# Casts and bank copies issued ahead of the exponentials in attention, and a transform's tiles loaded behind the modulation's row blocks

## The chip, the cores and the metric

One core of one Trainium2 chip runs the whole program in one launch. The metric is device microseconds per execution, the median over several runs. TensorE is written PE, its weight loads PEld, VectorE DVE, ScalarE ACT, GpSimd POOL and SyncE SP; the DMAs of this kernel are issued from SP's queue, in order.

## The reference, cut to what matters

One layer of a transformer-like block on 512 latent tokens (width 1024) and 256 context tokens, all in fp32:

```python
sh1, sc1, g1, sh2, sc2, g2 = split(silu(c) @ w_mod + b_mod, 6)      # and the same from c_ctx for the context
h  = rms_norm(x, norm1_g) * (1 + sc1) + sh1                          # hc likewise from ctx
qa, ka, va, hy, qd, kd, vd = split(h @ w_in)                         # ka, va, kd, vd of hc too
ya = attention(qa, [ka_c; ka], [va_c; va])                           # 4 heads of 64, 2 key heads, 768 keys
yd = softmax(q1 k1) v - lam * softmax(q2 k2) v                       # 4 heads, values 128 wide
yh = x2 * conv(h2, x1 * conv(h1, v))                                 # long convolutions by FFT, filters from a small MLP
x  = x + g1 * (concat(norm(ya), norm(yh), norm(yd)) @ w_out)
x  = x + g2 * conv_glu(rms_norm(x, norm2_g) * (1 + sc2) + sh2)       # up to 2 x 2816, down to 1024
```

Two details matter below. The modulation `silu(c) @ w_mod` has to be complete before the first row of h exists. The long convolution is done with matrices of cosines and sines ("dft" tiles), first on the filters (`spectrum("s", ..)` and `spectrum("d", ..)`), later on the data.

## The kernel before, in words

Nearly every product is done as three matmuls (`mm3`): both operands are split into a high part, made by a cast on ACT (`hi_of`, L72), and a remainder, made by a subtraction on DVE or POOL (`lo_of`, L80). The three matmuls then stand at L83, L84 and L85. A weight tile thus costs a DMA, a cast of 128x1024 and a subtraction of 128x1024.

**First stage (L376 to L490).** The first 2048 columns of `w_mod` come as eight row blocks of 1 MB (`mod1_load`, L165, tile `mraw`, four buffers). `mod1(k)` (L249) multiplies block k into one PSUM bank; between these calls PE builds the filters (`filter_part`) and adds up their norms (`filter_norm`, L425). PE's order is written out by hand here (`manual_schedule` for PE alone); the order on ACT, DVE, POOL and SP is set by a planner from estimated times when the program is built, as far as data, buffers and `issue_after` allow. `load_dft(g)` (L263) loads 512 KB of cosine and sine matrices and splits them at once. After `mod1(7)` the bank is copied, transposed (`modT`, L257) and made into columns (`modc`, `gs1`). Then x, normalised, is transposed in eight pieces (`transposed`, L360), each modulated (`hm`), cast and split into `hTh`, `hTl`; the spectra of the filter sum stand between the pieces, the first of them in two halves, one of them ahead of `mod1(7)` (L450). `shy` streams the weights of the Hyena projection (`prep` casts and splits one).

**Projections (L500 to L925).** Hyena, then the eight q, k, v blocks `corder`. `mod2_step` (L746) takes one step of the other four modulation vectors: a DMA of 512 KB and a multiply-add on DVE; after every eighth step 16 small matmuls (`mc`, L768) sum over partitions, one call later, since `pause` lets one call pass. `MOD_AT` says how many calls go ahead of each weight unit. In the last block (ci = 7) the first three steps of attention are already done between the matmuls (`early_step`), PE and DVE in hand-written order.

**Attention (L1163 to L1215).** 16 steps of differential attention, then 16 of the grouped one; a step is 128 queries of one head. The loop counter n runs from 3. For n below LATE = 16 a step has two halves jj (the two softmaxes). For each: `front` does the scores on PE into one of two score banks (`ps_s`, 128x768) and then `exp_of` (L779): a maximum on DVE, an exponential on ACT. Around it stand, in program order: `combine(n-1)` (the two reciprocals and the mixing on POOL), `advance()` (one step of each running generator: splitting q and k of the next head, normalising a finished head, transposing it), `transposes(n-3, half)` (three transposes on PE into a bank `ps_t`, three of these in all, and their copy out on ACT, tiles `at`), and `values(n-5)`. PE, DVE and ACT all run in this hand-written order, so an instruction waits for every earlier one of its own engine:

```python
held[n] = front(n, 0)()              # scores, maximum, exponential of half 0
if on(D_C): combine(n - D_C, held[n - D_C])
advance()
if on(D_T): transposes(n - D_T, held[n - D_T][0], 0)
held[n] += front(n, 1)()
if on(D_T): transposes(n - D_T, held.pop(n - D_T)[0], 1)
if on(D_V): values(n - D_V)
```

**Tail of attention (L1205 to L1215).** The last head has to be copied, transposed, normalised (`finish_a`, L1014) and transposed again (`yTa`), one piece per `advance()`. Between these PE has 24 units of the output projection (`accumulate`, three matmuls of 512 columns each); `TAIL` says how many go ahead of each `advance()`. `wo_unit` (L1130) loads and splits a tile of `w_out`; `WO_LO` names the engine of the subtraction, one letter per tile. Tiles 3 to 7 are traced after the hand-written part (L1231).

Of the kernel before, what the change touches and what calls it, by code (L numbers as in the profile page):

```python
# [16 lines left out]
P = 128  # L17
WO_LO = "ppppvvvv"
# [9 lines left out]
TAIL = (2, 0, 0, 0, 0, 0, 7, 0, 0, 2)  # L28
# [16 lines left out]
def block_kernel(tc, x, ctxt, small, ffs, wmod1, wmod2, whyd, wqkvd, woutd, wupd, wdownd,  # L45
# [217 lines left out]
    def load_dft(g):  # L263
        if g < 2:
            stage = qk.tile([P, 4, 256], F32, tag=("yhn", "qa")[g], bufs=1, name=f"dft_{g}").rearrange("p a c -> p (a c)")
        else:
            stage = wp.tile([P, 1024], F32, tag="wr", bufs=3, name=f"dft_{g}")
        st = stage.rearrange("p (m a f) -> p m a f", m=2, a=2)
        dma(st, dftd[2 * g:2 * g + 2].rearrange("m (a p) f -> p m a f", p=P))
        h = dfp.tile([P, 2, 2, 256], F32R, name=f"dfh{g}")  # L270
        l = dfp.tile([P, 2, 2, 256], F32R, name=f"dfl{g}")
        hi_of(h, st, "a")
        lo_of(l, st, h, "v" if g < 2 else "p")
        for j in range(2):
            dft[names[2 * g + j]] = (h[:, j], l[:, j])
# [121 lines left out]
    load_dft(0)  # L397
    dma(coef, coefd.rearrange("(m p) c -> p m c", p=P))
# [4 lines left out]
    mod1_load(6)  # L403
    loaded = mod1_load(7)
    load_dft(1)
# [44 lines left out]
    spectrum("s", 0, (1,))  # L450
# [9 lines left out]
    with tc.issue_after(last[0].ins):  # L460
        shy.prep(0)
    mv = mod1_columns()
    dft["coT"] = dft["co"]
    dft["soT"] = dft["so"]
# [5 lines left out]
    for v in range(2):  # L470
        V.scalar_tensor_tensor(gs1[:, v], modc[:, 8:16, v], 1.0, cols[:, C_N1:C_N1 + 8], ALU.add, ALU.mult)
# [6 lines left out]
    for n in range(NK):  # L478
        next(tr)
        if n == 0:  # L480
            spectrum("s", 0, (0,))
        if n in (1, 3, 5):
            spectrum("s", (n + 1) // 2)
        if n == 5:
            with tc.issue_after(last[3].ins):
                shy.prep(1)
# [18 lines left out]
    for u in range(6):  # L505
        wh, wl = shy.get(u)
        if u == 2:
            load_dft(2)
# [237 lines left out]
    def mod2_step():  # L746

        if m2s.pop("pause", False):
            return
# [14 lines left out]
        if k == NK - 1:  # L764
            def due(a=m2s["a"]):
                t0 = m2s["ps"](f"mc{g}")
                for i in range(NK):
                    T_.matmul(t0[:, 2 * i:2 * i + 2], a[:, i * P:(i + 1) * P], ones[:, 0:2], start=True, stop=True)  # L768
                V.tensor_tensor(mcol[:, g], t0[:, 0:16:2], cols[:, C_BM + 8 * g:C_BM + 8 * g + 8], ALU.add)
            m2s["due"], m2s["pause"] = due, True  # L770
# [7 lines left out]

    def exp_of(p_, mx, s, stat):  # L779
        V.tensor_reduce(mx, s[:, :768], AX.X, ALU.max, negate=True)  # L780
        S.activation(p_, s[:, :768], AF.Exp, bias=mx, scale=1.0, accum_out=stat)
# [10 lines left out]
    def early_step(e):  # L792
# [11 lines left out]
        mx = cst.tile([P, 1], F32, tag="mxe", bufs=2, name=f"mxe{n}{jj}")  # L804
        exp_of(p_, mx, s, state["st0"][:, n, jj:jj + 1])
# [11 lines left out]
    for ci, ch in enumerate(corder):  # L817
# [6 lines left out]
        for u in range(2):  # L824
# [8 lines left out]
            for b, bank in enumerate(banks):  # L833
                th, tl = (hTh, hTl) if b < 2 else (cTh, cTl)
                for j in range(2):
# [6 lines left out]
                    if ci == 7:  # L842
# [5 lines left out]
                        if e % 3 == 0:  # L848
                            mod2_step()
# [164 lines left out]
    def finish_a(b, yps):  # L1014
# [15 lines left out]
        if b == 1:  # L1030
# [4 lines left out]
            for b_ in range(2):  # L1035
                yv = yna[b_].rearrange("p a j d -> p a (j d)")
                V.tensor_tensor(yv, yv, sa[:, 2].unsqueeze(2).broadcast_to([P, 4, P]), ALU.mult)
# [9 lines left out]
    def front(n, jj):  # L1047
# [3 lines left out]
        if kind == "a":  # L1051
            if jj:
                return lambda: []
# [9 lines left out]
        def rest():  # L1063
            mx = att.tile([P, 1], F32, tag="mx", bufs=4, name="mx" + nm)
            p_ = att.tile([P, 768], F32, tag="p", bufs=7, name="p" + nm)
            exp_of(p_, mx, s, stat)
            return [p_]
# [62 lines left out]
    def wo_unit(n_):  # L1130
# [10 lines left out]
        lo_of(l, r, h, WO_LO[n_])  # L1141
# [23 lines left out]
    while n < len(steps) + D_V:  # L1165
# [10 lines left out]
        if late:  # L1176
# [4 lines left out]
            if n - 1 in waiting:  # L1181
                held[n - 1] = waiting.pop(n - 1)()
# [9 lines left out]
        else:  # L1192
            held[n] = front(n, 0)()
# [5 lines left out]
            held[n] += front(n, 1)()  # L1199
            if on(D_T):  # L1200
                transposes(n - D_T, held.pop(n - D_T)[0], 1)
            if on(D_V):
# [304 lines left out]
```

## Time and profile before

| | |
|---|---|
| median of 3 runs | 807.86 us (805.63 to 809.38) |
| the profiled execution | 807.56 us, its span 805.8 us |
| PE busy | 774.5 us (96% of the span) |
| DVE, ACT, POOL busy | 476.9, 317.8, 194.6 us |
| granted clock of PE, mean | 0.991 |
| moved by DMA | 93.68 MB |

The span is the time from the first to the last instruction of the profiled execution. A row of the timeline reads: start, duration, engine, line, operation, output<-input, shape, count, and in square brackets how long the engine stood idle before it and which instruction ended that. Several equal instructions in a row are merged into one.

### The profile page before, as it was taken

The numbers are of one execution on the slowest core, as the hardware profiler recorded it, in microseconds if no ns is written. First come the engines' busy times: TensorE is split into PE (matmuls) and PEld (weight loads), VectorE is DVE, ScalarE is ACT, GpSimd is POOL, SyncE is SP. The second block draws the span as 40 slices with busy tenths as digits, with TensorE's granted clock in tenths as the row PEclk, the third lists the DMA queues.
The fourth block names the chain that finished last, engine by engine and source line by source line (L and its number), as shares of the span: only waits on it lengthen the run. The fifth ranks groups of instructions, "written<-read, shape, count | busy, mean of one in ns | idle before, by whom it ended". The sixth has DMA issues, their size and how long they took to land.

```text
span 805.8 us, 11143 instructions
## 1 busy us (share of the span) xinstructions
PE 774.5 (96%) x4355; PEld 655.1 (81%) x4355; DVE 476.9 (59%) x683; ACT 317.8 (39%) x546; POOL 194.6 (24%) x187
## 2 busy tenths in 40 slices
PE   8899999999989888899899999999999999999997
PEld 2278899999988777789689988888888888888886
DVE  5588659687767777776476785344444433332325
ACT  2576343223213678787243343323333332332220
POOL 0518036849821657421151000000000000000000
PEclk9799999999999999999999999999999999999999
DMA  8913311225675241501551372322232222223202
GB/s 325 393 51 112 105 54 53 79 79 179 214 218 161 66 104 29 144 27 53 171 171 54 113 245 86 105 104 83 101 105 90 93 99 84 100 85 104 79 27 104
DMA packets 30701, 93.68 MB, mean 116 GB/s; under 512 B 5639, under 2 KB 8022, under 8 KB 29625
## 3 DMA queue, kind: packets, MB, share of 16 engines
q1 hardware_dynamic: 30649, 92.98, 35.0%
q8 instruction: 34, 0.56, 0.3%
q14 instruction: 18, 0.15, 0.1%
HBM read 83.79 MB, written 2.10 MB: 107 GB/s over the span
## 4 chain that ended last, share of the span: by engine, by line
PE 81%; DVE 6%; DMA 4%; ACT 4%; POOL 2%; issue 1%; SPq 0%; ACTq 0%; DVEq 0%; POOLq 0%
PE u L84 5%; PE u L83 5%; PE u L85 5%; PE dn L85 5%; PE dn L84 5%; PE dn L83 5%; DMA mraw<-in_dram 4%; PE uv L83 2%; PE ua L85 2%; PE uv L84 2%; PE uv L85 2%; PE ua L83 2%; PE ua L84 2%; PE yd L1103 2%; PE o L85 2%; PE o L84 2%
## 5 line engine op out<-in xcount | busy, mean ns | idle before, releaser
L80 DVE TENSOR_TENSOR ul<-ur,uh 128x1024 fp32r<-128x1024 f32 x62 | 75.9, 1224 | 101.6 <-ACT uh L72 100.9
L72 ACT CAST uh<-ur 128x1024 fp32r<-128x1024 f32 x66 | 69.2, 1051 | 116.8 <-PE u L84 90.6
L83 PE MATMUL u<-h2h,uh 128*128 128x512 f32 (+1 forms) x224 | 81.3, 363 | 0.0
L85 PE MATMUL u<-h2h,ul 128*128 128x512 f32 (+1 forms) x224 | 80.4, 359 | 0.0
L84 PE MATMUL u<-h2l,uh 128*128 128x512 f32 (+1 forms) x224 | 80.4, 359 | 0.0
L84 PE MATMUL dn<-ul,gh 128*128 128x512 f32 x176 | 69.6, 397 | 0.0
L85 PE MATMUL dn<-uh,gl 128*128 128x512 f32 x176 | 69.6, 397 | 0.0
L83 PE MATMUL dn<-uh,gh 128*128 128x512 f32 x176 | 69.3, 397 | 0.0
L80 DVE TENSOR_TENSOR gl<-gT,gh 128x512 fp32r<-128x512 f32 x22 | 15.2, 690 | 60.1 <-ACT gh L72 60.1
L84 PEld LDWEIGHTS u<-h2l,uh 128*128 128x128 f32 x224 | 42.3, 189 | 6.3
L83 PEld LDWEIGHTS u<-h2h,uh 128*128 128x128 f32 x224 | 42.3, 189 | 6.2
L85 PEld LDWEIGHTS u<-h2h,ul 128*128 128x128 f32 x224 | 42.3, 189 | 6.2
L80 DVE TENSOR_TENSOR wl<-wr,wh 128x1024 fp32r<-128x1024 f32 x22 | 31.5, 1433 | 19.4 <-ACT wh L72 19.3
L763 DVE SCALAR_TENSOR_TENSOR macc<-mraw,sv,macc 128x1024 f32<-128x1024 f32 x28 | 37.4, 1335 | 8.1 <-DMA mraw<-in_dram 8.0
L72 ACT CAST gh<-gT 128x512 fp32r<-128x512 f32 x22 | 13.5, 620 | 70.1 <-PE dn L84 70.1
L83 PEld LDWEIGHTS dn<-uh,gh 128*128 128x128 f32 x176 | 33.2, 189 | 8.1
L85 PEld LDWEIGHTS dn<-uh,gl 128*128 128x128 f32 x176 | 33.2, 188 | 8.1
L84 PEld LDWEIGHTS dn<-ul,gh 128*128 128x128 f32 x176 | 33.2, 188 | 8.0
L72 ACT CAST wh<-wr 128x1024 fp32r<-128x1024 f32 x22 | 23.0, 1047 | 41.2 <-PE hy L84 8.2
L83 PE MATMUL uv<-h2h,uh 128*128 128x512 f32 x80 | 31.2, 391 | 0.2 <-ACT uh L72 0.2
L83 PE MATMUL ua<-h2h,uh 128*128 128x512 f32 x80 | 31.4, 392 | 0.0
L84 PE MATMUL uv<-h2l,uh 128*128 128x512 f32 x80 | 31.2, 390 | 0.0
(771 smaller groups left out, 2173.9 us busy)
## 6 DMA issues: line engine op xcount, KB each, us to landing
ur<-in_dram SPq DMA_DIRECT2D x66, 512.0 KB, 3.2
mraw<-in_dram SPq DMA_DIRECT2D x32, 512.0 KB, 4.5
wr<-in_dram SPq DMA_DIRECT2D x22, 512.0 KB, 3.3
mraw<-in_dram SPq DMA_DIRECT2D x8, 1024.0 KB, 11.8
or<-in_dram SPq DMA_DIRECT2D x8, 512.0 KB, 4.6
xo<-in_dram SPq DMA_DIRECT2D x6, 512.0 KB, 9.3
x<-in_dram SPq DMA_DIRECT2D x4, 512.0 KB, 5.8
out_dram<-x SPq DMA_DIRECT2D x8, 256.0 KB, 2.0
```

What stands on the lines that cost most here:

```text
L72: return S.copy(dst, src)
L80: return e.tensor_tensor(dst, src, f(hi), ALU.subtract)
L83: i0 = T_.matmul(o, ah, bh, start=start, stop=False)
L84: T_.matmul(o, ah, bl, start=False, stop=False)
L85: return i0, T_.matmul(o, al, bh, start=False, stop=stop)
L763: V.scalar_tensor_tensor(m2s["a"], r, sv[:, k:k + 1], m2s["a"], ALU.mult, ALU.add)
L1103: T_.matmul(o, Vt[2 + h][:, kt], at[:, kt], start=kt == 0, stop=kt == 5)
```

## The change

In the first stage it loads the two dft pieces later (the first behind row block 6, the second behind block 7), puts six matmuls on a zero tile where half of the first spectrum stood, and does the spectra whole, one behind every second transposed piece. In the modulation's second part it pauses one call longer after the second vector and moves the calls inside the last projection block. In attention it parts the maximum from the exponential: copies and casts traced between now go first on ACT. In the tail it gives 10 and 4 units where 7 and 2 stood, puts tile 3's subtraction on DVE, and holds the subtractions of tiles 4 to 7 behind the last scaling of the last head.

```diff
-WO_LO = "ppppvvvv"
+WO_LO = "pppvvvvv"
...
-TAIL = (2, 0, 0, 0, 0, 0, 7, 0, 0, 2)
+TAIL = (2, 0, 0, 0, 0, 0, 10, 0, 0, 4)
...
-        dma(st, dftd[2 * g:2 * g + 2].rearrange("m (a p) f -> p m a f", p=P))
+        dft["dma"] = dma(st, dftd[2 * g:2 * g + 2].rearrange("m (a p) f -> p m a f", p=P))
         h = dfp.tile([P, 2, 2, 256], F32R, name=f"dfh{g}")
         l = dfp.tile([P, 2, 2, 256], F32R, name=f"dfl{g}")
-        hi_of(h, st, "a")
-        lo_of(l, st, h, "v" if g < 2 else "p")
...
+        def split():
+            hi_of(h, st, "a")
+            lo_of(l, st, h, "v" if g < 2 else "p")
...
+        return split
...
     mod1_load(3)
-    load_dft(0)
-    dma(coef, coefd.rearrange("(m p) c -> p m c", p=P))
     mod1_load(4)
     for a in (2, 3):
         x_load(a)
     mod1_load(5)
-    mod1_load(6)
-    loaded = mod1_load(7)
-    load_dft(1)
+    loaded = mod1_load(6)
+    with tc.issue_after(loaded.ins):
+        split = load_dft(0)
+    with tc.issue_after(dft["dma"].ins):
+        split()
+        loaded = mod1_load(7)
+    with tc.issue_after(loaded.ins):
+        dma(coef, coefd.rearrange("(m p) c -> p m c", p=P))
+        split = load_dft(1)
+    loaded = dft["dma"]
...
-    spectrum("s", 0, (1,))
+    warm(6, "3")
     mod1(7)
...
-    with tc.issue_after(last[0].ins):
-        shy.prep(0)
...
-        V.scalar_tensor_tensor(gs1[:, v], modc[:, 8:16, v], 1.0, cols[:, C_N1:C_N1 + 8], ALU.add, ALU.mult)
+        ins = V.scalar_tensor_tensor(gs1[:, v], modc[:, 8:16, v], 1.0, cols[:, C_N1:C_N1 + 8], ALU.add, ALU.mult)
+    with tc.issue_after(ins.ins):
+        split()
...
         next(tr)
-        if n == 0:
-            spectrum("s", 0, (0,))
-        if n in (1, 3, 5):
-            spectrum("s", (n + 1) // 2)
-        if n == 5:
+        if n % 2:
+            spectrum("s", n // 2)
+        if n in (3, 5):
             with tc.issue_after(last[3].ins):
-                shy.prep(1)
+                shy.prep(n // 2 - 1)
...
-        if m2s.pop("pause", False):
+        if m2s.get("pause"):
+            m2s["pause"] -= 1
             return
...
-            m2s["due"], m2s["pause"] = due, True
+            m2s["due"], m2s["pause"] = due, 2 if g == 1 else 1
...
+    def max_of(mx, s):
+        V.tensor_reduce(mx, s[:, :768], AX.X, ALU.max, negate=True)
+
     def exp_of(p_, mx, s, stat):
-        V.tensor_reduce(mx, s[:, :768], AX.X, ALU.max, negate=True)
         S.activation(p_, s[:, :768], AF.Exp, bias=mx, scale=1.0, accum_out=stat)
...
-                        if e % 3 == 0:
+                        if e in (2, 4, 6, 8, 9):
                             mod2_step()
...
-                V.tensor_tensor(yv, yv, sa[:, 2].unsqueeze(2).broadcast_to([P, 4, P]), ALU.mult)
+                state["yna"] = V.tensor_tensor(yv, yv, sa[:, 2].unsqueeze(2).broadcast_to([P, 4, P]), ALU.mult)
...
         hi_of(h, r, "a")
-        lo_of(l, r, h, WO_LO[n_])
+        if n_ < 4:
+            lo_of(l, r, h, WO_LO[n_])
+        else:
+            with tc.issue_after(state["yna"].ins):
+                lo_of(l, r, h, WO_LO[n_])
...
-                held[n - 1] = waiting.pop(n - 1)()
+                held[n - 1] = waiting.pop(n - 1)()()
...
-            held[n] = front(n, 0)()
+            exps = front(n, 0)()
             if on(D_C):
                 combine(n - D_C, held[n - D_C])
             advance()
             if on(D_T):
                 transposes(n - D_T, held[n - D_T][0], 0)
-            held[n] += front(n, 1)()
+            held[n] = exps()
+            exps = front(n, 1)()
             if on(D_T):
                 transposes(n - D_T, held.pop(n - D_T)[0], 1)
+            held[n] += exps()
             if on(D_V):
                 values(n - D_V)
```

`issue_after(ins)` adds an edge of order from `ins` to each instruction traced in its block that runs on the engine of `ins`, and to no other. In the first stage the edges thus bind SP's queue alone, at the second split DVE alone. `front` now returns the scores' continuation in two calls, the first for the maximum, the second for the exponential; the steps from n = 16 on call both at once, as before.

## Rows read from the trace of the kernel before

**Rows 1.** The busy time of each engine in stretches of the span: length, then PE, PEld, DVE, ACT, POOL, the granted clock of PE, the DMA share and GB/s.
```profile
0.00:50.00 50.00, 41.57 (x160) 15.86 (x161) 31.25 (x60) 22.08 (x44) 12.88 (x23) 0.90 0.82 302
50.00:200.00 150.00, 150.00 (x1065) 140.22 (x1064) 113.70 (x165) 57.07 (x95) 81.14 (x81) 1.00 0.26 88
...
226.00:268.00 42.00, 38.29 (x298) 37.19 (x296) 27.91 (x39) 12.56 (x24) 8.24 (x7) 0.96 0.61 175
268.00:330.00 62.00, 51.51 (x314) 44.42 (x314) 46.82 (x87) 45.64 (x103) 40.66 (x33) 1.00 0.34 82
...
376.00:401.00 25.00, 22.70 (x122) 18.76 (x122) 10.00 (x15) 7.58 (x11) 3.61 (x3) 1.00 0.36 127
```

**Rows 2.** The timeline of PE in the first stage: matmuls on a zero tile (`warm`), filters (`f`), row blocks and norms (`modl`), the half spectrum (`ktC0s`, first row of six matmuls).
```profile
10.35 1.88 PE L205 MATMUL warm<-nil 128*128 128x448 bf16 x9
...
26.91 1.98 PE L413 MATMUL f<-fw3s,h 65*128 65x512 f32 x4
32.38 1.93 PE L251 MATMUL modl<-mraw,scol 128*32 128x512 f32 x8 [3.48 <-DMA mraw<-in_dram]
34.24 3.59 PE L425 MATMUL modl<-habs,ones 128*128 128x512 f32 x4
...
38.76 1.13 PE L425 MATMUL modl<-habs,ones 128*128 128x512 f32 x2
39.33 0.80 PE L83 MATMUL ktC0s<-fhsp,dfh 128*128 128x512 f32 x1
...
41.21 1.07 PE L251 MATMUL modl<-mraw,scol 128*32 128x512 f32 x8
```

**Rows 3.** A stretch of the first stage by itself, columns as in rows 1.
```profile
30.00:38.00 8.00, 5.62 (x16) 1.53 (x20) 4.32 (x6) 4.51 (x12) 5.11 (x8) 0.57 1.01 415
```

**Rows 4.** The timeline of SP's queue: when DMAs were issued (the duration is that of the issue, not of the transfer).
```profile
18.05 0.43 SPq L269 DMA_DIRECT2D dft<-in_dram  x1
18.58 4.35 SPq L168 DMA_DIRECT2D mraw<-in_dram  x3
...
37.34 0.38 SPq L619 DMA_DIRECT2D rope<-in_dram  x1
```

**Rows 5.** The timelines of ACT and DVE in the first stage: the cast and the subtraction of the first Hyena weight tile.
```profile
44.48 1.06 ACT L72 CAST wh<-wr 128x1024 fp32r<-128x1024 f32 x1
...
45.57 1.22 DVE L80 TENSOR_TENSOR wl<-wr,wh 128x1024 fp32r<-128x1024 f32 x1 [0.17 <-ACT wh L72]
```

**Rows 6.** The timeline of PE from 233 to 253 us: its waits in the last projection blocks.
```profile
236.49 1.92 PE L768 MATMUL mc<-ones,macc 128*128 128x2 f32 x16 [2.11 <-DVE macc L763]
247.68 0.50 PE L776 MATMUL se<-ks1d,qsd 128*128 128x512 f32 x1 [0.55 <-ACT pe L781]
252.54 0.50 PE L776 MATMUL se<-ks0d,qsd 128*128 128x512 f32 x1 [1.05 <-ACT pe L781]
```

**Rows 7.** DVE around the last of these waits, and the stretch behind the first of them (columns as in rows 1).
```profile
249.25 1.28 DVE L763 SCALAR_TENSOR_TENSOR macc<-mraw,sv,macc 128x1024 f32<-128x1024 f32 x1 [1.46 <-DMA mraw<-in_dram]
250.46 0.95 DVE L780 TENSOR_REDUCE mxe<-se 128x1 f32<-128x768 f32 x1
...
236.00:247.00 11.00, 10.51 (x74) 10.39 (x74) 7.32 (x11) 2.96 (x4) 0.00 (x0) 0.84 0.48 150
```

**Rows 8.** The timeline of PE in attention: the waits that ended with a copy or cast on ACT, and one of those that ended with an exponential (the first row).
```profile
271.45 0.50 PE L776 MATMUL sd10None<-ksX,X 128*128 128x512 f32 x1 [0.76 <-ACT pd03None L781]
...
279.17 0.55 PE L1086 MATMUL Td02None<-ident,pe 128*128 128x128 f32 x3 [1.21 <-ACT atd02None L72]
285.26 0.55 PE L1086 MATMUL Td03None<-ident,pd03None 128*128 128x128 f32 x3 [1.77 <-ACT atd02None L72]
...
311.17 0.55 PE L1086 MATMUL Td21None<-ident,pd21None 128*128 128x128 f32 x3 [1.67 <-ACT atd20None L72]
316.70 0.55 PE L1086 MATMUL Td22None<-ident,pd22None 128*128 128x128 f32 x3 [1.20 <-ACT ynd L991]
...
327.86 0.55 PE L1086 MATMUL Td31None<-ident,pd31None 128*128 128x128 f32 x3 [1.06 <-ACT atd30None L72]
329.12 0.66 PE L971 MATMUL yTd<-ident,ynd 128*128 128x128 f32 x4 [0.71 <-ACT atd30None L72]
```

**Rows 9.** ACT's queue in one of these steps, ahead of the wait at 285.26, and one row of a later step (a finished head's square).
```profile
282.74 0.90 ACT L781 ACTIVATE pd12None<-sd12None,mxd12None 128x768 f32<-128x768 f32 x1 [2.36 <-DVE mxd12None L780]
...
283.63 0.47 ACT L72 CAST khd<-kT1d 128x384 fp32r<-128x384 f32 x1
283.99 0.85 ACT L978 ACTIVATE Y<-yTh,cols 128x256 fp32r<-128x256 f32 x2
284.71 0.50 ACT L72 COPY atd02None<-Td03None 128x384 f32<-128x384 f32 x1
...
298.25 0.63 ACT L992 ACTIVATE ysqd<-ynd 128x512 f32<-128x512 f32 x1
```

**Rows 10.** The tail of attention: PE's first matmul of the seven units, its two waits, and the subtraction that DVE does ahead of the last head's sums.
```profile
382.02 0.48 PE L83 MATMUL o<-oh,Y 128*128 128x512 f32 x1
...
388.61 0.63 PE L971 MATMUL yTa<-ident,yna 128*128 128x128 f32 x4 [1.44 <-DVE yna L1037]
...
391.49 0.63 PE L971 MATMUL yTa<-ident,yna 128*128 128x128 f32 x4 [0.85 <-DVE yna L1037]
...
382.98 2.59 DVE L80 TENSOR_TENSOR ol<-or,oh 128x1024 fp32r<-128x1024 f32 x1
...
```

More of the change, by code (lines that the diff above doesn't have):

```diff
@@ L268, in load_dft @@
         st = stage.rearrange("p (m a f) -> p m a f", m=2, a=2)
-        dma(st, dftd[2 * g:2 * g + 2].rearrange("m (a p) f -> p m a f", p=P))
+        dft["dma"] = dma(st, dftd[2 * g:2 * g + 2].rearrange("m (a p) f -> p m a f", p=P))
         h = dfp.tile([P, 2, 2, 256], F32R, name=f"dfh{g}")
         l = dfp.tile([P, 2, 2, 256], F32R, name=f"dfl{g}")
-        hi_of(h, st, "a")
-        lo_of(l, st, h, "v" if g < 2 else "p")
-        for j in range(2):
-            dft[names[2 * g + j]] = (h[:, j], l[:, j])
+        def split():
+            hi_of(h, st, "a")
+            lo_of(l, st, h, "v" if g < 2 else "p")
+            for j in range(2):
+                dft[names[2 * g + j]] = (h[:, j], l[:, j])
+        return split
     ss = cst.tile([P, 6], F32, name="ss1")
@@ L459, in block_kernel @@
         shy.load(1)
-    with tc.issue_after(last[0].ins):
-        shy.prep(0)
     mv = mod1_columns()
-    dft["coT"] = dft["co"]
-    dft["soT"] = dft["so"]
     modc = cst.tile([P, 16, 2], F32, name="modc")
@@ L470, in block_kernel @@
     for v in range(2):
-        V.scalar_tensor_tensor(gs1[:, v], modc[:, 8:16, v], 1.0, cols[:, C_N1:C_N1 + 8], ALU.add, ALU.mult)
+        ins = V.scalar_tensor_tensor(gs1[:, v], modc[:, 8:16, v], 1.0, cols[:, C_N1:C_N1 + 8], ALU.add, ALU.mult)
+    with tc.issue_after(ins.ins):
+        split()
+    dft["coT"] = dft["co"]
+    dft["soT"] = dft["so"]
     close(raw1)
@@ L507, in block_kernel @@
         if u == 2:
-            load_dft(2)
+            load_dft(2)()
         wh, wl = (w.rearrange("p (k c) -> p k c", k=NK) for w in (wh, wl))
@@ L804, in early_step @@
         mx = cst.tile([P, 1], F32, tag="mxe", bufs=2, name=f"mxe{n}{jj}")
+        max_of(mx, s)
         exp_of(p_, mx, s, state["st0"][:, n, jj:jj + 1])
@@ L1052, in front @@
             if jj:
-                return lambda: []
+                return lambda: lambda: []
             stat, j_ = sta[:, tt, 2 * h + j:2 * h + j + 1], j
@@ L1064, in rest, with exps @@
             mx = att.tile([P, 1], F32, tag="mx", bufs=4, name="mx" + nm)
-            p_ = att.tile([P, 768], F32, tag="p", bufs=7, name="p" + nm)
-            exp_of(p_, mx, s, stat)
-            return [p_]
+            max_of(mx, s)
+            def exps():
+                p_ = att.tile([P, 768], F32, tag="p", bufs=7, name="p" + nm)
+                exp_of(p_, mx, s, stat)
+                return [p_]
+            return exps
         return rest
```

## The prediction

> **What bounds the kernel now.** I read the stretches first [rows 1]: PE is full from 50 to 200 us (150.0 of 150.0) and PE busy time is nearly the whole span, so only PE's idle time, and time at its lower clock, can be won. The stretches show where it lies: 8.4 us in the first 50 us, 3.7 us from 226 to 268, 10.5 us from 268 to 330 (the differential attention), 2.3 us from 376 to 401 (its tail). Then I read, for each, which wait ends PE's idleness. In the first stage it is the modulation's sixth row block (block 5): PE waits 3.48 us for it, until 32.38, and then goes on slowly, since the granted clock has fallen [rows 2, 3]. In the last projection block it is a multiply-add and two exponentials [rows 6]. In attention it is ACT, almost always a copy out of a transpose bank [rows 8]. In the tail it is DVE's scaling of the last head [rows 10]. The change touches each of the four. No term lies in the PE-full stretch; what comes earlier ahead of it passes through it whole, as PE has no wait there that could take it back.
>
> **First stage.** In the before the second dft load is issued at 18.05, ahead of blocks 5 to 7 [rows 4]; the first one went out before that. The change puts both behind block 6. The DMAs are then saturated (415 GB/s, share 1.01 [rows 3]), so what counts is the bytes ahead of a block: 2 x 0.524 MB less at 415 GB/s make blocks 5 and 6 land 2.5 us earlier, and block 7, which still has the first dft ahead, 1.3 us earlier. Block 5: 32.4 to 29.9. PE is through with the filters at 28.9 [rows 2], so the gap shrinks from 3.5 to 1.0 us.
>
> With so short a gap I take the clock to stay up. The rows price both levels: the same eight matmuls took 1.93 us behind the gap and 1.07 at 41.21, two norm matmuls 1.13 at 38.76 and four 3.59 behind the gap [rows 2]. At the full clock: block 5 29.9 to 31.0, four norm matmuls (1.8, half of 3.59) to 32.8; block 6 is there by then, to 33.9; the last norm (1.1) to 35.0; six matmuls on the zero tile at 1.88 / 9 each (1.3) to 36.3. When does block 7 land? The issue of rope, which the queue held for one of these blocks, went out at 37.34 [rows 4]; I read 37.3 for block 7, so 36.0 after. `mod1(7)` runs 36.3 to 37.4, where it ended at 42.3: 4.9 us gained.
>
> From this goes back what moves: half of the first spectrum, six matmuls, stood between 39.33 and 41.21 [rows 2] and now stands behind the modulation, on the path. At the pace of the 512-column units in the tail (21 in 5.15 us, below) it costs 1.4 us. A short wait of the old order inside it (part of the first matmul's 0.80) goes: 0.4. Net 3.9 us. The dft's second split (a cast of 1.06 and a subtraction of 1.22, by the weight tile of the same size [rows 5]) moves into the stretch of the transposed pieces, and the split of a Hyena weight tile of the same price moves out of its start, to the fourth piece; both lie beside the eight pieces and four spectra. The weight tile is wanted only after the last spectrum; without that cover the two cost 2.3. Behind the held dft loads on SP stand coef, three Hyena tiles, gains and rope; coef is wanted at the first spectrum's end, the tiles at the fourth piece, all some us after they land. POOL's queue is not passed. Bounds: 1.3 (clock stays low, below) to 4.9.
>
> **Last projection block.** The wait of 1.05 us for an exponential [rows 6] comes from DVE: the maximum at 250.46 stood behind a multiply-add that waited 1.46 us for its DMA [rows 7]. After the change the steps come at e = 2, 4, 6, 8, 9, behind the maxima traced at the same e. I take that wait as gone, the one of 0.55 as kept: 1.0. The fifth step taken in there adds 1.28 us to DVE, which has 14 us idle in the 42 [rows 1]; nobody waits but the last vector's sum, whose last step stays at e = 9. Bounds: 0 to 1.6. The second pause puts the call that sums the second vector one later, but the two calls stand directly behind one another ahead of the same weight unit (`MOD_AT` gives 2), so PE gets no work between them: I cost it at nothing, with the wait of 2.11 us [rows 6] kept. If it went, so would the low clock behind it, 16% of 11 us [rows 7], together 3.9 us; so its bounds are 0 and 3.9, and nothing here lengthens it.
>
> **Attention.** Six waits on copies make 7.6 us [rows 8]. One of them step by step [rows 9]: PE waits until 285.26 for the copy at 284.71. Ahead of that copy ACT did an exponential (282.74 to 283.63), a k cast (to 283.99) and a Y pair (to 284.71). ACT stood idle for 2.36 us before the exponential, until the maximum was there; the k and Y transposes stood behind the scores on PE, as the maximum did, and a maximum takes 0.95 us [rows 7]. In the new order the k cast starts while the maximum runs. The copy comes earlier by the exponential's 0.89 and by some 0.6 of the idle time: 1.5 of the 1.77. Taken over the six, some 0.3 us each is left: 5.8 gained. Two things go the other way. The exponential starts up to the casts' 1.1 us later in steps with k and Y, and its score bank is wanted again by the next step's scores: PE comes back to it after two groups of transposes, one of scores and one of values, about 2.8 us on these steps (a step is 62 / 13 = 4.8 us, 4.0 of it busy [rows 1], less its own scores and the running pieces). Maximum and exponential need 0.95 + 0.90, so 0.9 us is spare, which most casts fit. In the two steps in which a finished head's copy and square (0.6 and 0.63 [rows 9]) and the bank's copy go first, it is passed by about 0.5 each: 1.0 lost. Net 4.8. DVE's order is unchanged except that its reciprocals wait for an exponential that may be later; they have the rest of the step. Bounds: 0 (the waits change their name) to 7.6.
>
> **Tail.** Seven units took from 382.02 to 388.61 - 1.44, 0.73 each [rows 10]; ten take until 389.3. The scaling they wait for ended at 388.5, so the wait of 1.44 goes even if DVE is no faster; four units in place of two cover 0.85 as well. All units remain, only fewer at the end (8 for 13), still 5.7 us ahead of those that need the last head. In the before DVE's subtraction of a weight tile took 2.59 us [rows 10] where the same size takes 1.22 alone [rows 5]; it shares that time with POOL's. Tile 3's now runs on DVE by itself, and tiles 4 on wait for the scaling, which helps the sums but no longer sets anything. Tile 4's buffer comes free some 7 us later, so the last w_out tile is loaded later on SP, and x behind it; both are wanted more than 10 us after. 2.2 us, bounds 1.4 to 2.3.
>
> **The sum.** 3.9 + 1.0 + 4.8 + 2.2 = 11.9 us off the profiled execution's 807.56 (span 805.8 and 1.76 around it): 795.7. That execution lies 0.3 below the median of the runs, 807.86, so I forecast 796.0.
>
> **Rivals.** *The clock stays low.* Behind block 3, too, PE was idle and slow, and the clock was 0.57 in the mean from 30 to 38 us [rows 3]. If it falls in a 1.0 us gap as well, block 5 takes 1.93 and the norms 3.59, `mod1(7)` ends near 40.0, and the stage gives 2.3 less the 1.0 that goes back, 1.3: 798.6. For it: the matmuls around the gap are few. Against it: in attention single gaps of up to 1.77 us [rows 8] lie in a stretch with a clock of 1.00 [rows 1]. [...]
>
> *The waits change their name.* Every copy PE no longer waits for is replaced by a score bank not yet free (as at 271.45, 0.76 us [rows 8]): attention gives nothing, 800.8. Against it: ACT is busy 45.6 of the 62 us [rows 1], so it can catch up.
>
> *The second pause does its work.* The sum's wait and the slow clock behind it go: 3.9 us more, 792.1.
>
> *Slower: the score banks decide.* If ACT always had a copy and a q cast to do (0.36 and 0.46) when the maximum ends, and PE came back earlier than the exponential in all 26 halves, PE would lose 26 x 0.82 = 21.3 us in place of the 1.0 above: 816.3. It decides once maximum, casts and exponential together exceed PE's 2.8 us in every half; the rows show that only in the steps named.
>
> **How the numbers follow.** Forecast 0.55, low clock 0.18, waits renamed 0.12, second pause 0.11, slower 0.04. About 0.5% (4 us, below 803.8) is what a measurement of this kernel can tell from no change. The first, second and fourth lie below that, 0.84; of the third a part, since with a low clock it passes to 803.4 and any small loss carries it over: 0.04 of it faster, 0.08 the same. So faster 0.88, same 0.08, slower 0.04. The range reaches from the second pause (792.1, and some 0.6 for attention's upper bound) to 802.0, past the renamed waits; outside stay the slower case, the far part of the third and a few hundredths below.
>
> **What would show it.** In the changed profile: block 5's wait under 1.5 us and PE's clock at 1.0 from 24 us on, the bank's transpose near 38 us; from 268 to 330 an idle time of about 6 us of PE where 10.5 stood, none of its waits on a copy over 0.6 us; the two waits at `yTa` gone. I am wrong if PE's waits on exponentials in attention come to over 4 us, if block 5 still ends a gap of over 2.5 us, or if a new PE wait appears between 50 and 226 us, where the planner orders ACT, DVE and SP anew.

## The result, and the profile after

| | median us | lowest to highest | runs | ratio to before | 95% interval |
|---|---|---|---|---|---|
| before | 807.75 | 805.63 to 809.38 | 12 | 1 | |
| after | 799.66 | 795.99 to 807.66 | 12 | 0.9915 | 0.9894 to 0.9936 |

The change takes 8.1 us off the median (a second measurement, e11, has 0.9909). 796.0 was forecast, 11.9 less than the 807.86 us known then. The execution profiled after took 796.37 us (span 794.6), 11.2 less than the one profiled before. It is one of the faster ones: the median of the runs of after lies 3.3 us above it. Those runs go over 12 us where those of before go over 4, and time follows the mean granted clock (795.99 us at 0.995, 799 at 0.993, 803.46 at 0.983, 807.66 at 0.975).

The stretches of after, columns as in [rows 1]:

```profile
0.00:50.00 50.00, 43.31 (x185) 18.44 (x186) 33.43 (x64) 26.54 (x51) 18.37 (x24) 1.00 0.79 292
50.00:200.00 150.00, 148.74 (x1058) 139.18 (x1057) 112.60 (x164) 54.80 (x92) 82.73 (x83) 1.00 0.28 95
226.00:268.00 42.00, 38.42 (x288) 36.88 (x286) 28.52 (x41) 12.91 (x26) 10.46 (x7) 0.94 0.56 165
268.00:330.00 62.00, 58.18 (x353) 50.31 (x352) 49.54 (x93) 51.37 (x113) 42.91 (x35) 0.98 0.38 96
376.00:401.00 25.00, 25.00 (x118) 20.31 (x117) 13.87 (x18) 10.15 (x16) 4.71 (x4) 1.00 0.53 189
```

PE's idle time in attention's stretch fell from 10.5 to 3.8 us (from the first scores to `sa`, the same work in both, from 10.47 to 3.89), the tail's from 2.3 to nothing. (The 1.26 us missing in the second row are PE's wait for a weight cast, 1.25 us in before, where it lay behind 200 us.) For sizes, the first matmuls of the same tiles are compared, before less after, each difference the gain up to there:

| PE's first matmul on | before | after | gain |
|---|---|---|---|
| `modT`, the modulation's transpose | 43.03 | 36.76 | 6.27 |
| `ktC1s`, the second spectrum | 46.48 | 44.37 | 2.11 |
| `q0L`, the first projection | 103.83 | 100.86 | 2.97 |
| `q6L` / `q7L`, before and behind the second vector | 219.17 / 241.73 | 216.20 / 239.68 | 2.97 / 2.05 |
| the first scores in attention proper | 268.36 | 264.88 | 3.48 |
| `sa`, the end of the differential heads' share | 330.73 | 322.18 | 8.55 |
| `u`, behind the tail | 430.89 | 419.67 | 11.22 |

**First stage.** PE, answering [rows 2]:

```profile
27.67 1.07 PE L251 MATMUL modl<-mraw,scol 128*32 128x512 f32 x8 [0.78 <-DMA mraw<-in_dram]
28.67 1.98 PE L433 MATMUL modl<-habs,ones 128*128 128x512 f32 x4
...
35.00 1.06 PE L251 MATMUL modl<-mraw,scol 128*32 128x512 f32 x8 [1.05 <-DMA mraw<-in_dram]
36.76 0.66 PE L257 MATMUL modT<-ident,msb 128*128 128x128 f32 x4 [0.70 <-ACT msb L461]
...
39.05 0.76 PE L368 MATMUL xT<-ident,xo 128*128 128x128 f32 x5 [1.31 <-POOL xo L298]
...
41.60 0.50 PE L84 MATMUL ktC0s<-flsp,dfh 128*128 128x512 f32 x1 [0.85 <-DVE flsp L80]
...
44.37 0.48 PE L83 MATMUL ktC1s<-fhsp,dfh 128*128 128x512 f32 x1
```

The row blocks come as forecast or earlier and the clock is 1.00. But 6.27 us gained at `modT` are 2.11 at the second spectrum: PE waits for POOL and for DVE. DVE in the same time:

```profile
32.85 0.68 DVE L454 SCALAR_TENSOR_TENSOR hbias<-modl,hbias 1x512 f32<-1x512 f32 x1 [2.57 <-PE modl L433]
33.46 1.20 DVE L80 TENSOR_TENSOR dfl<-dft,dfh 128x1024 fp32r<-128x1024 f32 x1
34.59 0.67 DVE L455 SCALAR_TENSOR_TENSOR sd<-hf,hbias 1x512 f32<-1x512 f32 x1
35.19 0.67 DVE L80 TENSOR_TENSOR flsp<-fpsp,fhsp 128x512 fp32r<-128x512 f32 x1
35.80 0.67 DVE L80 TENSOR_TENSOR flsm<-fpsm,fhsm 128x512 fp32r<-128x512 f32 x1
...
39.01 1.21 DVE L80 TENSOR_TENSOR dfl<-dft,dfh 128x1024 fp32r<-128x1024 f32 x1
...
41.47 0.68 DVE L80 TENSOR_TENSOR flsm<-fpsm,fhsm 128x512 fp32r<-128x512 f32 x1
```

Behind the last norm (the bias sum `hbias`) DVE works without a gap until the fold's last subtraction. Before, the same two rows stood 4.8 us apart, with DVE idle for 4.61 ahead of them:

```profile
39.93 0.68 DVE L446 SCALAR_TENSOR_TENSOR hbias<-modl,hbias 1x512 f32<-1x512 f32 x1 [4.61 <-PE modl L425]
...
44.71 0.69 DVE L80 TENSOR_TENSOR flsm<-fpsm,fhsm 128x512 fp32r<-128x512 f32 x1
```

Both dft splits (1.20, 1.21; at 23.7 and 30.5 before) and the first fold's subtractions (0.67 each; at 34.0 and 34.6) had been done ahead of the norm; now they lie in this row of work, 3.84 us longer than before.

**Second vector and early steps.** PE at the wait of [rows 6], and the clock behind it:

```profile
234.14 2.06 PE L775 MATMUL mc<-ones,macc 128*128 128x2 f32 x16 [2.73 <-DVE macc L770]
```
```profile
236.00:238.00 2.00, 2.00 (x10) 2.00 (x11) 1.53 (x3) 0.00 (x0) 0.00 (x0) 0.50 0.29 115
238.00:240.00 2.00, 2.00 (x14) 2.00 (x14) 0.58 (x1) 0.13 (x1) 0.00 (x0) 0.71 0.77 262
```

The second pause did not take the wait away (2.73 us for 2.11), and time at the lower clock stays with it (0.50 from 236 to 238 us, 0.71 from 238 to 240). PE came 2.97 us earlier, and 0.9 of it is lost here: the multiply-adds on DVE ahead of the sum wait for their own DMAs (2.87 and 0.75 us), so a PE that comes earlier waits longer. In e11, a second execution of the same program, PE comes 4.0 us later than in after, waits 0.85 us and is 2.0 us later behind it.

**Attention.** All of PE's waits from 268 to 330 us that come to 0.3 us or more (total, times, longest), and ACT's queue where [rows 9] showed it:

```profile
PE yTd L981 <- ACT atd30None L72: 1.7, 1, 1.7
PE sd32None L783 <- ACT pd31None L790: 0.7, 1, 0.7
PE sd11None L783 <- ACT pd10None L790: 0.6, 1, 0.6
PE Td02None L1100 <- ACT atd02None L72: 0.3, 1, 0.3
PE Td03None L1100 <- ACT atd02None L72: 0.3, 1, 0.3
```
```profile
278.39 0.48 ACT L72 CAST khd<-kT1d 128x384 fp32r<-128x384 f32 x1 [0.80 <-PE kT1d L706]
278.83 0.84 ACT L988 ACTIVATE Y<-yTh,cols 128x256 fp32r<-128x256 f32 x2
279.56 0.48 ACT L72 COPY atd02None<-Td03None 128x384 f32<-128x384 f32 x1
279.92 0.92 ACT L790 ACTIVATE pd12None<-sd12None,mxd12None 128x768 f32<-128x768 f32 x1
```

The cast, the Y pair and the copy now go ahead of the exponential, and the 1.77 us of [rows 8] is 0.27. One wait is missing here that the other traces with this attention have. In e3, where the clock is 1.00 throughout:

```profile
PE sd10None L776 <- ACT pd03None L783: 0.7, 1, 0.7
```

It is 0.9 us in e5, e9 and e11 and 1.2 in e12. In after the clock is 0.57 from 266 to 270 us; PE takes 3.57 us from the first scores to `sd10` (e3: 3.04, the wait included) and does not wait there.

**Tail.** DVE, answering [rows 10]: the subtraction of 2.59 us takes 1.22, and PE's two `yTa` groups start without a wait.

```profile
382.55 0.68 DVE L1047 TENSOR_TENSOR yna<-yna,sa 128x512 f32<-128x512 f32 x1
383.15 1.22 DVE L80 TENSOR_TENSOR ol<-or,oh 128x1024 fp32r<-128x1024 f32 x1
```

### The profile page after: what moved, and what is told of

The parts are those of the page before. It is cut to its first block, busy times and chain, and to the rows that moved or that the text cites. A ratio compares the mean times of both kernels' runs of the same rounds, so it can differ in the third digit from the quotient of the medians.

```text
span 794.6 us, 11153 instructions
## 1 busy us (share of the span) xinstructions
PE 774.2 (97%) x4361; PEld 656.0 (83%) x4361; DVE 475.3 (60%) x684; ACT 319.1 (40%) x546; POOL 197.2 (25%) x186
## 4 chain that ended last, share of the span: by engine, by line
PE 81%; DMA 6%; DVE 5%; ACT 3%; POOL 2%; SPq 2%; issue 1%; DVEq 0%; ACTq 0%; POOLq 0%
PE u L84 5%; PE u L83 5%; PE u L85 5%; PE dn L85 5%; PE dn L84 5%; PE dn L83 5%; DMA mraw<-in_dram 5%; PE uv L83 2%; PE ua L85 2%; PE uv L85 2%; PE uv L84 2%; PE ua L83 2%; PE ua L84 2%; PE yd L1117 2%; PE o L85 2%; PE o L84 2%
```

## The experiments

Four kernels take the change apart (e1 to e4 ran together, e5 to e8 together, e9 to e11 together, e12 by itself, each time beside the kernel before).

**e1, the first stage alone.** All of the diff's first-stage pieces, nothing else:

```diff
...
-    load_dft(0)
...
+    with tc.issue_after(loaded.ins):
+        split = load_dft(0)
...
-    spectrum("s", 0, (1,))
+    warm(6, "3")
...
```

> The first stage's part alone (loads, six matmuls on a zero tile, whole spectra), all else as before. Forecast's theory: 3.9 us faster than before, 803.9; the trace of the whole change lets me expect 2.9 at the start of the second projection block, so 804.8. If the whole change's wide scatter (796.0 to 807.7, with a mean clock of 0.995 to 0.975) came from the shifted first stage, the scatter and the low clock appear here: runs up to 11 us above the fastest. If it comes from attention, the scatter here stays as before's (under 4 us).

**e2, the modulation steps alone.**

```diff
...
-            m2s["due"], m2s["pause"] = due, True
+            m2s["due"], m2s["pause"] = due, 2 if g == 1 else 1
...
-                        if e % 3 == 0:
+                        if e in (2, 4, 6, 8, 9):
```

> The modulation's steps alone (second pause, calls at e = 2, 4, 6, 8, 9). Forecast's theory: 1.0 us faster, 806.8, the wait of 2.1 us for the second vector's sum unchanged. Rival (the second pause does its work): 3.9 us more, 802.9. If the 0.5 us that the whole change's trace shows is all there is: 807.3. Scatter as before's.

**e3, attention alone.**

```diff
...
-            held[n] += front(n, 1)()
+            held[n] = exps()
+            exps = front(n, 1)()
...
```

> Attention's part alone (maximum and exponential parted, copies and casts first). Forecast's theory: 4.8 us faster, 803.0, with PE idle about 5 us from 268 to 330 us where 10.5 stood. Rival (waits change their name): 807.8. Theory of the low clock in attention: scatter up to 11 us above the fastest, with mean clocks down to 0.975, the fastest run near 803, and the median some 2 to 3 us above it. Theory that the scatter is not attention's: all runs within 4 us.

**e4, the tail alone.**

```diff
-WO_LO = "ppppvvvv"
+WO_LO = "pppvvvvv"
...
-TAIL = (2, 0, 0, 0, 0, 0, 7, 0, 0, 2)
+TAIL = (2, 0, 0, 0, 0, 0, 10, 0, 0, 4)
...
+            with tc.issue_after(state["yna"].ins):
+                lo_of(l, r, h, WO_LO[n_])
```

> The tail's part alone (10 and 4 units, tile 3's subtraction on DVE, tiles 4 to 7 held back). Forecast's theory: 2.2 us faster, 805.6, both waits at yTa gone. Scatter as before's, clock unchanged.

| | median us | ratio | 95% interval | off 807.11 |
|---|---|---|---|---|
| e1 first stage | 809.46 | 1.0043 | 1.0016 to 1.0070 | +2.4 |
| e2 modulation steps | 806.67 | 0.9992 | 0.9973 to 1.0011 | -0.4 |
| e3 attention | 800.73 | 0.9924 | 0.9901 to 0.9948 | -6.4 |
| e4 tail | 804.49 | 0.9970 | 0.9948 to 0.9993 | -2.6 |

The four sum to -7.0, the whole change gives -8.1. Attention and the tail gave more than forecast (4.8 and 2.2); the first stage, forecast at -3.9, is slower by itself; e2's step can't be told from nothing. The spread shows in two of the four: e1's runs go over 10.2 us (clocks 0.979 to 0.995) and e3's over 9.0 (one run at 0.984, the others over 4.4), e2's and e4's over 5.2 and 6.8, as the 31 of before beside them do (6.8). In e1's trace PE is 1.14 us early at `q0L`, and the second vector's wait takes that back and more:

```profile
236.34 3.22 PE L774 MATMUL mc<-ones,macc 128*128 128x2 f32 x16 [3.12 <-DVE macc L769]
```

From `q6L` to `q7L` it takes 25.4 us, before 22.6; the same stretch took 20.9 in e4 (wait 1.1) and 23.8 in e3 (3.0), neither of which touches anything ahead of it. So this place by itself moves by several us between executions; the next step tests whether it is the cause.

**e5, all but the first stage.** The diff of e1 taken out of the whole change.

> Everything of the change except the first stage. The whole change measured 0.9915 of the time before (799.7 us), the first stage by itself 1.0043 (2.4 us slower). Theory A, the first stage costs time also in company: this run lies below the whole change, at 0.988 to 0.990 (797 to 798.5 us). Theory B, the first stage gives the 3.0 us that the trace of the whole change shows up to 216 us, and its loss when alone came from the wait for the second modulation vector behind it: this run lies above, at 0.993 to 0.996 (801.5 to 804 us).

797.93 us, 0.9882 (0.9861 to 0.9904), the runs from 796.7 to 799.22. That is as theory A had it: in company too the first stage seems to cost some 2 us (the interval just overlaps that of the whole change), and without it the spread is 2.5 us.

**e6, the second vector's sum later; e7, the same without the first stage.** Made to the whole change (e6) and to e5's kernel (e7):

```diff
-MOD_AT = (0, 0, 0, 2, 2, 2, 2, 2, 2, 2, 2, 2, 2, 2, 0, 0)
+MOD_AT = (0, 0, 0, 2, 2, 2, 2, 2, 2, 2, 2, 2, 0, 0, 0, 0)
...
-            m2s["due"], m2s["pause"] = due, 2 if g == 1 else 1
+            m2s["due"], m2s["pause"] = due, 1
...
-                        if e in (2, 4, 6, 8, 9):
+                        if e in (1, 2, 3, 4, 5, 6, 8, 9):
```

> The whole change, with the sum of the second modulation vector (the 16 two-column matmuls) moved from the end of the sixth projection block into the seventh, behind its second group of matmuls, some 4 us later on TensorE; the eight steps of the third vector then come at e = 1, 2, 3, 4, 5, 6, 8, 9. Theory A, the wait of 2.1 to 3.1 us for that vector and the half clock behind it are what eats the first stage's gain: both go, the clock is 1.00 from 230 to 264 us, and the time falls by 3 to 4 us, to 0.987 of the time before (796 us), with less scatter. Rival B, TensorE only takes the wait elsewhere (eight loads of rows in a shorter time, the third vector's sum late at the block's end): 0.990 to 0.993, and the trace shows a longer wait of the sum near 264 us. Rival C, the scatter of the runs comes from elsewhere: time falls by 1 to 2 us and the spread of 10 us stays.

> The change without the first stage, and with the second vector's sum moved as in the other kernel. With its pair it prices the first stage free of that wait. Theory A, the first stage gains 2 to 3 us once nothing behind it takes them back: this kernel is 2 to 3 us slower than the one with the first stage, about 0.990 to 0.991 of the time before. Rival, the first stage gives nothing or costs in itself (its two splits on VectorE lie on the path): the same time or up to 2 us faster, 0.985 to 0.987.

e6: 801.65 us, 0.9929 (0.9902 to 0.9956); e7: 798.70, 0.9891 (0.9867 to 0.9914). The wait of [rows 6] went, and as rival B had it PE waits elsewhere: for an exponential, more than for the third vector's sum. e6's waits of PE, then its stretches up to and behind 247 us:

```profile
PE se L783 <- ACT pe L790: 2.2, 1, 2.2
PE mc L775 <- DVE macc L770: 0.8, 1, 0.8
```
```profile
226.00:247.00 21.00, 21.00 (x173) 20.59 (x173) 12.70 (x15) 6.38 (x10) 1.14 (x2) 1.00 0.55 155
247.00:268.00 21.00, 17.53 (x126) 16.72 (x125) 16.32 (x22) 6.20 (x13) 6.40 (x4) 0.92 0.65 186
```

The eight steps stand between the maxima and PE waits for an exponential; the clock falls there instead (0.92). And the pair prices the first stage as before: with it 801.65, without it 798.70. With the second vector's wait gone from both, the first stage still costs time by the medians (the intervals overlap a little), so that wait is not the main part of what eats its gain. The two profiled executions are alike (798.48 and 798.56): the difference is in the spread, 798.48 to 807.89 in e6 and 797.17 to 799.64 in e7.

**e8, the fold ahead of the second split.** To the whole change:

```diff
-    with tc.issue_after(ins.ins):
+    with tc.issue_after(last[1].ins):
         split()
```

> The whole change, with the second dft's split on VectorE behind the fold's two subtractions, where it stood ahead of them (nothing else moves but one ScalarE cast by one place). Theory A, VectorE is what sets the first stage now (it is busy without a gap from 32.9 to 42.7 us, and TensorE waits 0.85 us for the fold): the wait goes, the Hyena projections start 0.85 to 1.2 us earlier, and the time falls by 0.8 to 1.2 us, 0.990 of the time before. Rival B, the next thing on the path takes its place (the x rows on GpSimd, the second spectrum's own wait for the split): TensorE waits as long for that, no difference.

797.23 us, 0.9889 (0.9854 to 0.9924): too wide to tell from the whole change. In its trace the wait for the fold is gone, but PE waits 3.25 us for POOL's last x rows (rival B), since an instruction on one column (0.19 elsewhere) stood in POOL for 4.67 us while DVE worked through its row. In after it was the scaling itself, 5.36 us beside that row; in e11 it ended as the row began, and took 1.12:

```profile
33.98 4.67 POOL L296 TENSOR_TENSOR ss<-sx 128x1 f32<-128x1 f32 x1
```
```profile
33.64 5.36 POOL L298 TENSOR_SCALAR xo<-xo,rs 128x1024 f32<-128x1024 f32 x1
```
```profile
35.00 1.12 POOL L298 TENSOR_SCALAR xo<-xo,rs 128x1024 f32<-128x1024 f32 x1
```

**e9, more matmuls on the zero tile; e10, none of the six; e11, the whole change again.**

```diff
+        if n == 3:
+            warm(6, "4")
         mod1(n + 2)
...
     mod1(7)
+    warm(3, "5")
...
+        if n == 1:
+            warm(6, "6")
```
```diff
-    warm(6, "3")
     mod1(7)
```

> The whole change with 15 more 448-column matmuls on the zero tile in the gaps of the first stage: 6 ahead of block 5, 3 behind block 7, 6 ahead of the first spectrum (1.3, 0.65 and 1.3 us at the full clock, each into a wait that the traces show: 0.8 to 2.3 us, 0.7 us, 1.3 to 3.3 us). Theory A, the runs above 800 us are runs in which the clock falls in the gaps of the new first stage and stays low in its spectra: the slow runs go, the median falls to 796.5 to 797.5 (0.987 to 0.988 of before) and the mean clock is 0.99 or more in nearly every run. Rival B, the low clock comes from elsewhere (the wait for the second vector, attention): the spread of 796 to 808 and the median stay, or the added matmuls cost up to 1 us.

> The whole change without its six matmuls on the zero tile ahead of block 7 (1.3 us, in a place where TensorE waits 1.05 us longer still). Theory A, gaps in the first stage bring the low clock: the gap there grows to some 2.4 us, more runs fall, the median rises by 2 to 5 us to 801.5 to 805 (0.993 to 0.997 of before) and mean clocks of 0.975 to 0.985 are common. Rival B, the low clock comes from elsewhere: the median stays within 0.7 us of the whole change (799.7), or 1 us lower.

> The whole change once more, beside the two others on the same chip. Both theories expect its 799.7 us (796 to 808) again. Should the profiled execution have a mean clock of 0.985 or less, theory A expects its low clock between 25 and 60 us, and rival B between 230 and 330 us.

| | median us | lowest to highest | mean clocks | ratio | 95% interval |
|---|---|---|---|---|---|
| e9 | 797.82 | 795.21 to 801.32 | 0.991 to 0.998 | 0.9885 | 0.9857 to 0.9912 |
| e10 | 797.48 | 794.67 to 798.23 | 0.990 to 0.994 | 0.9873 | 0.9849 to 0.9898 |
| e11 | 799.31 | 797.18 to 803.27 | 0.984 to 0.993 | 0.9909 | 0.9881 to 0.9937 |

The clocks of e9 rose as theory A said; e10's median did not rise as it said: without the six matmuls nothing got slower. The three intervals overlap, so the medians do not rank the three. Nor is e10 a clean test: the planner laid DVE out anew, with a pair of the first fold's subtractions ahead of the norm again, as in before:

```profile
31.67 0.69 DVE L80 TENSOR_TENSOR flsp<-fpsp,fhsp 128x512 fp32r<-128x512 f32 x1 [1.05 <-ACT fhsp L72]
```

The gap ahead of block 7 did grow, to 2.12 us, and the lower clock followed (0.50 from 36 to 40 us, `mod1(7)` 1.94 us for 1.06), and yet PE stands at 100.97 at `q0L`, 2.86 earlier than before. In e9 too DVE's order is another. So what the gaps are worth for the spread stays open. e11's trace, the same program as after, shows what can differ inside the stage. PE, then DVE, then the stretches at 30 and 44 us:

```profile
29.37 1.06 PE L251 MATMUL modl<-mraw,scol 128*32 128x512 f32 x8 [1.57 <-DMA mraw<-in_dram]
30.37 3.67 PE L433 MATMUL modl<-habs,ones 128*128 128x512 f32 x4
...
44.17 0.79 PE L84 MATMUL ktC0s<-flsp,dfh 128*128 128x512 f32 x1 [2.28 <-DVE flsp L80]
...
48.41 0.48 PE L83 MATMUL ktC1s<-fhsp,dfh 128*128 128x512 f32 x1
```
```profile
36.13 0.68 DVE L454 SCALAR_TENSOR_TENSOR hbias<-modl,hbias 1x512 f32<-1x512 f32 x1 [4.48 <-PE modl L433]
...
44.04 0.68 DVE L80 TENSOR_TENSOR flsm<-fpsm,fhsm 128x512 fp32r<-128x512 f32 x1
```
```profile
30.00:34.00 4.00, 4.00 (x14) 1.21 (x9) 1.65 (x3) 2.80 (x9) 2.69 (x5) 0.57 1.05 385
44.00:48.00 4.00, 3.83 (x12) 3.06 (x13) 1.44 (x4) 1.44 (x3) 2.21 (x1) 0.57 0.01 2
```

Block 5 landed later, the norms ran slowly (3.67 us for 1.98, the clock 0.57 from 30 to 34 us), DVE's row began 3.3 us later, PE waited 2.28 us for it, and the clock was low a second time behind that wait (0.57 from 44 to 48 us, matmuls of 512 columns 0.63 us). (In e1 and e6 PE waits 2.29 and 2.28 us at the same place, and the clock stays at 1.00 from 44 to 48 us; in e1 such matmuls take 0.39 to 0.40.) The second spectrum starts 4.0 us later than in after, 1.9 later than before. Laid side by side:

| execution | block 5's wait | bias sum | to the fold's last subtraction | second spectrum | gain there | at `q0L` |
|---|---|---|---|---|---|---|
| before | 3.48 | 39.93 | 4.78 | 46.48 | 0 | 0 |
| after | 0.78 | 32.85 | 8.62 | 44.37 | 2.11 | 2.97 |
| e1 | 2.29 | 35.37 | 7.91 | 46.19 | 0.29 | 1.14 |
| e6 | 2.33 | 35.96 | 7.91 | 46.78 | -0.30 | 0.56 |
| e11 | 1.57 | 36.13 | 7.91 | 48.41 | -1.93 | -1.08 |

DVE's row is 7.91 us three times, whatever came ahead (8.62 in after, where the two small `gs` instructions, beside POOL's scaling, took 0.95 for 0.24 to 0.25 in the three). The gain is the earlier bias sum less 3.1 for the longer row, less 1.1 for the half spectrum behind it: for e1 4.56 - 3.13 - 1.14 = 0.29. The mean of the four at `q0L` is 0.9; the six traces with the old stage lie at 0 to 0.7 there, 0.4 in the mean. By these traces the stage is worth about 0.5 us, where the medians of e1, e5 and the pair e6 and e7 say that it costs 2 to 3. The profiled executions of the stage are at or below the medians of their kernels (796.37, 809.43, 798.48 and 797.77 for 799.66, 809.46, 801.65 and 799.31), and e1's trace loses its gain behind `q6L`; the rest of the difference may lie in executions that no trace shows.

**e12, two moves of the first stage taken back.** e8's edit, and:

```diff
-    warm(6, "3")
+    spectrum("s", 0, (1,))
...
-            spectrum("s", n // 2)
+            spectrum("s", n // 2, (0,) if n == 1 else (1, 0))
```

> The whole change with its loads, but with two of its moves in the first stage taken back: the half of the first spectrum stands ahead of block 7 again (in place of the six matmuls on the zero tile), and the second dft's split stands behind the fold on VectorE. Theory A, what sets the stage is VectorE's row of instructions from the last norm to the fold (7.9 us from the bias sum to the last subtraction in three traces, 4.8 before the change), and the half spectrum behind it (1.1 us): from the bias sum to the second spectrum's first matmul it takes 8.5 us where the whole change took 10.8 to 12.3, the Hyena projections start at 53 to 56 us, the time falls 1.5 to 2.3 us below the whole change, to 797 to 798 (0.987 to 0.988 of before). Rival B, the half spectrum now waits for the first fold ahead of block 7, and the modulation and the x pieces come late in its place: the same 10.5 us or more, 799 to 801 us.

795.50 us, 0.9838 (0.9809 to 0.9868), the runs from 791.52 to 796.49 at clocks of 0.993 to 0.999: below the whole change's interval, and the lowest median here (the interval still touches those of e5 and e7 to e10). PE and DVE:

```profile
28.88 1.93 PE L251 MATMUL modl<-mraw,scol 128*32 128x512 f32 x8 [2.19 <-DMA mraw<-in_dram]
...
38.82 0.50 PE L85 MATMUL ktC0s<-fhsp,dfl 128*128 128x512 f32 x1 [1.44 <-DVE dfl L80]
...
46.22 0.48 PE L83 MATMUL ktC1s<-fhsp,dfh 128*128 128x512 f32 x1
```
```profile
36.95 0.68 DVE L454 SCALAR_TENSOR_TENSOR hbias<-modl,hbias 1x512 f32<-1x512 f32 x1 [4.07 <-PE modl L433]
...
44.12 0.68 DVE L80 TENSOR_TENSOR flsm<-fpsm,fhsm 128x512 fp32r<-128x512 f32 x1
```

This execution had the latest bias sum of all with the new loads, and yet its second spectrum starts at 46.22: 9.3 us behind it, where the new stage took 10.8 to 12.3. That bears theory A out in direction (8.5 forecast). It does not isolate DVE's row: the planner put a pair of the first fold's subtractions back ahead of the norm here too, and DVE is no longer busy throughout but stands for 1.39 us until the modulation's transpose is there:

```profile
42.41 0.19 DVE L470 TENSOR_TENSOR modc<-modT,cols 128x32 f32<-128x32 f32 x1 [1.39 <-PE modT L257]
```

From the bias sum to the last subtraction it takes 7.17 us (7.91 in e1, e6 and e11), and 0.8 less from there to the second spectrum. PE's wait of 1.44 us for the first split, ahead of block 7, is of rival B's kind. The Hyena projections start at 56.5, just outside the 53 to 56 expected, and PE's gain at `q0L` is 1.0, within what the other traces have. The median fell by more (3.8 us below e11, 3.4 when each is taken off the runs of before beside it) than the 1.5 to 2.3 expected. The trace does not hold that gain (795.94 us, after's 796.37); the runs' clocks are higher throughout, and how that comes of the edit is not shown.

## Why the prediction was right, and where it was not

The time lay in the range (796.0 forecast, 791.5 to 802.0, measured 799.66), by terms of which two were too small and one was nearly empty; in part that is luck. Taken alone, attention and the tail gave 2.0 us more than forecast (9.0 for 7.0) where the first stage gave 6.3 less (-2.4 for 3.9). The median lies nearer to the 798.6 of the low clock and the 800.8 of the renamed waits than to 796.0, but not by the second of these mechanisms, and by the first only in some executions.

- **First stage, 3.9: the step that failed.** What it said of the row blocks held: `mod1(7)` ran at 35.0 (36.3 forecast), PE's path up to `modT` gained 6.27 (4.9), the half spectrum cost 1.1 (1.4). It failed at "both lie beside the eight pieces and four spectra". The prediction named the price without that cover, 2.3, and did not ask what DVE had to finish ahead of the first spectrum. The fold waits on DVE behind the last norm, and both dft splits and the first fold's subtractions were put into that row: 3.1 us more. By the traces the bias sum, not the modulation, became the start of the stage's longest chain; e12 agrees with that but does not isolate it. Up to `q0L` the stage gave 3.0 us in one trace and -1.1 to 1.1 in three others; by the medians it costs 2.4 us alone and about 2 in company. The "short wait" of 0.4 in the old half spectrum is in no row: the first matmul's 0.80 has no idle time ahead of it.
- **"I take the clock to stay up".** It did in after's trace. In e1 and e6 a gap of 2.3 us at block 5 and in e11 one of 1.57 were followed by the lower clock, in norms and matmuls that now lie on the chain (block 5's matmuls 1.93 us in e1 and 1.94 in e6 for 1.07 in after, the norms 2.55, 2.56 and 3.67 in e1, e6 and e11 for 1.98). The rival with the low clock forecast 1.3 us for the stage, nearer to these three than the likeliest case. It counted the low clock's own cost, not the longer row.
- **Early steps, 1.0.** From `q7L` to attention 25.2 us in place of 26.6: 1.4, and within 0.05 of that in e2 and e5 as well. "At nothing" for the second pause held. "Nothing here lengthens it" did not: the wait went from 2.11 to 2.73 us, because PE came 2.97 us earlier and the last multiply-add, behind its DMA, only 2.35 (232.71 for 235.06); with the clock behind it 0.92 us of the first stage's gain stayed there. That what comes earlier "passes through it whole" is true of the PE-full stretch (2.97 us at `q0L` and at `q6L`), but not of what lies behind it.
- **Attention, 4.8.** 5.1 us in the trace of after, 6.3 in e3's, 6.4 as e3's median (in after's the clock is 0.57 from 266 to 270 us, behind the third vector's two-column matmuls, and PE's busy time is 1.5 us longer than before; in e3's the clock is 1.00 from 268 to 330). Five of the six copy waits of [rows 8] fell to 0.3 or less. The sixth, `yTd`, grew from 0.71 to 1.7; none over 0.6 was expected. So in e3 the copies gave 5.1 where 5.8 was forecast. The waits for exponentials grew from 1.3 (`sd10`, `sd11`, `sd33`: 0.8, 0.3, 0.2) to 2.0 in e3 and 2.2 to 2.5 in e5, e9, e11 and e12: 0.7 to 1.2, near the loss of 1.0, and well under the 4 of a wrong forecast; only after's own trace, slow at `sd10`, shows 1.3. The surplus is in smaller waits that the forecast did not count and that are gone: 0.6, 0.4, 0.4 and 0.2, 1.6 us in all. Idle time in e3 fell by 6.0, which is 5.1 + 1.6 - 0.7. Neither the renamed waits nor the deciding score banks came.
- **Tail, 2.2.** 2.7 in the trace, 2.6 as e4's median; both waits went, and DVE's subtraction fell from 2.59 to 1.22 (in before POOL's of 2.41, from 382.08, ran beside it; in after POOL has none there).
- **The sum, 11.9.** The trace has 11.22 (2.97 - 0.92 + 1.43 + 5.07 + 2.67), the median 8.1. The prediction put the clock's level into one rival and did not allow for a spread between executions. Of the 37 runs with the first stage as changed 9 have a mean clock of 0.985 or less, of 109 with the old stage (before, e2 to e5, e7) 6. Where the low clock lies in those runs, and whether it comes of the stage, is open: no execution below 0.987 was profiled.

## What to carry to other kernels

When work is moved "beside" other work, look at the queue that does it and at what else that queue owes to the path: an engine that idles ahead of a sum can be a full chain behind it (DVE in e11: 4.48 us idle ahead of the bias sum, 7.91 us of work without a gap behind it). When a gain shows on one engine's path (6.3 us at `modT`), follow it to the next point at which two paths meet before booking it. When a planner orders an engine, look in the trace at what else an edit moved before reading its time as the edit's. And take a part that is fed by DMA and sits on a changing clock from several executions, not from one trace.

## What the runs showed of the hardware

- Identical programs put block 5's end of wait at 27.67 and 29.37 us, and the start of the second spectrum at 44.37 and 48.41: a 1.7 us difference in landing grew to 4.0 with a low clock in e11 from 30 to 34 us (0.57; norms 1.98 and 3.67 us) and again from 44 to 48 us (0.57), behind PE's 2.28 us wait.
- In e7 the stretch from 25 to 35 us ran at a granted clock of 0.50 with PE busy throughout, and its Hyena projections still began at 56.3, 0.8 earlier than in before, whose clock was 0.78 in that stretch and whose PE stood for 3.48 us of it waiting for a DMA: in these two executions the start was not later at the lower clock.
- Beside DVE's unbroken row POOL's scaling of 128x1024 took 5.36 us (after) and an addition on one column 4.67 (e8); with DVE idle they took 1.12 and 0.19 (e11).
